# The last gate piece of a hybrid attention step, multiplied inside the first attention blocks

## The chip, the cores and the metric

The kernel runs on one core of one Trainium2 chip. The metric is device time in microseconds. The time before is 711.84 us, the median of three runs (711.51 to 711.89).

A core has five engines with a queue each. TensorE (PE in the profile) multiplies matrices into PSUM; its weight loads stand in a row of their own (PEld). VectorE (DVE), ScalarE (ACT) and GpSimd (POOL) do elementwise work; SyncE (SP) issues most of the transfers. Each engine takes its instructions in the order in which the program wrote them.

## The reference

One layer of a diffusion backbone for 128 context tokens and 1024 latent tokens, with 1024 channels. A normalized and modulated input h goes through one projection, whose columns are the queries, keys, values and gates of two mixers. Mixer A attends globally, mixer B in a window of 128 with a learned sink. Each mixer's output is multiplied by the SiLU of its gate, and both go through one output projection:

```
p = h @ w_in
q_a, k_a, v_a, g_a, q_b, k_b, v_b, g_b = jnp.split(p, SPLIT_IDX, axis=-1)
...
jnp.concatenate([o_a * jax.nn.silu(g_a), o_b * jax.nn.silu(g_b)], axis=-1) @ w_out
```

All of it is float32, and the kernel gets its accuracy by splitting an operand into a high and a low part: a product is then three matmuls (high x high, low x high, high x low).

## The kernel before

**Stages.** The kernel modulates and turns the input (h stays in SBUF as 2 x 3 x 8 pieces: high and low, three groups of tokens of 512, 256 and 384 columns, eight slices of 128 channels), multiplies the gates of mixer A, the queries, the keys and values, and then the gates of mixer B. After that comes the attention, with the output projection woven in.

**The gates of mixer B.** `gates` (L301) goes through 12 pieces: for each of the three token groups four pieces of 128 gate columns. A piece is 24 matmuls (`gate_products`, L253: eight slices times three) into one PSUM bank. `block` (L268) calls `tick` twice in a piece; `tick` (L131) runs what was put down with `later`. One tick behind its end a piece's SiLU runs on ScalarE, and SyncE stores the result in DRAM (`put_gates`, L286, into `g_dram`). The first four pieces are made at L842; the loop at L1060 makes the other eight. Beside these eight, at an even rate set in L1050, run 26 steps that find the score maxima of attention units 0 and 2 (L881, with the reduction on VectorE at L882), and the splits of w_out into high and low (`split_wo`, L1033) at set ticks (`WO_STEPS`, L53). The last gate piece holds the gate columns 384 to 511 of mixer B for the token columns 768 to 1151; the attention reads it for its last tokens only.

**The attention.** After a table load on ScalarE (L1069) the loop at L1262 goes through slots, here called blocks. A unit is one query tile, one mixer and one pair of heads. A unit of mixer A has nine blocks, one of mixer B three or four. Block s writes the scores of block s (`scores`, L1107) and the values of block s - 3 (`values`, L1134); between the two stand the steps that fall due: score maxima for a later unit of mixer A (L881), masked scores for the next unit of mixer B (L938 to L942, with their exponential at L928), weight splits, and products of the output projection (`out_items`, L1199), which start with block 23. In mixer A a block is: two matmuls for the scores (L1120, L1121), an exponential on ScalarE (L1123), the cast to the high part on ScalarE (L1127), the low part by a subtraction on GpSimd (L1131; every ninth on VectorE, L1129), and three matmuls with the values (L1141, L1143, L1144). In mixer B the weights are turned by four transposes (L1115), and cast and subtraction are L1116 and L1117.

**Buffers that make engines wait.** Scores alternate between two PSUM banks (tag B), score maxima, masked scores and small transposes between two others (tag A), the value sums between two (tag C); D and E belong to the output projection. A bank is free when its readers are done.

**The 1/denominator of mixer B** goes through a small reciprocal on VectorE (L977), a transpose on TensorE (L990), a copy on ScalarE (L994) and DRAM. For mixer A it is a logarithm and an exponential on ScalarE (L1155, L1156), one block after the unit's last value product, and the product on VectorE three blocks later (L1165).

**Places in SBUF.** The pieces of h are given up behind the gates, and w_out takes their places: `wo_big` and `spare` are the third group of tokens (L1030, L1074). The parts of w_out with the numbers 12 and 13 are loaded at blocks 8 and 9 and split three blocks later (`WO_LATE`, L51; loop L1266). `ogp` (L1079) holds the high and low parts of the gated outputs, five buffers each.

**Order.** `in_order` (L94) ties every instruction to the one before it on its engine, so the order of the code is that of the engines.

Of the kernel before, what the change touches and what calls it, by code (L numbers as in the profile page):

```python
# [9 lines left out]
F32 = mybir.dt.float32  # L10
F32R = mybir.dt.float32r
BF16 = mybir.dt.bfloat16
AF = mybir.ActivationFunctionType
ALU = mybir.AluOpType
# [4 lines left out]
P = 128  # L19
D = 1024  # L20
KT = D // P
# [26 lines left out]
MX_END = 10  # L48
SPLIT_LAG = 2

WO_LATE = {12: 8, 13: 9, 11: 21, 14: 22, 15: 23}  # L51

WO_STEPS = ((0, 4, 4), (1, 5, 5), (2, 6), (3, 7), (4, 8, 6), (5, 9), (6, 11), (7, 12, 10), (8, 13), (9, 14), (10, 16))  # L53
TURN = 2
# [9 lines left out]
NOG = 5  # L64
# [24 lines left out]
def place(t):  # L89

    return (t - 1) % NT
# [17 lines left out]
def hybrid_step(ctx, tc, x_prompt, x_sample, cache_k_a, cache_v_a, cache_k_b, cache_v_b,  # L109
# [3 lines left out]
    nc = tc.nc  # L113
# [6 lines left out]
    g_dram = dram.tile([16 * HD, TOK], F32, name="gd")  # L120
    gate_row = dram.tile([2, D], F32, name="gate_row")
# [5 lines left out]
    def later(n, f):  # L127

        agenda.setdefault(now[0] + n, []).append(f)

    def tick():  # L131
        now[0] += 1
        for f in agenda.pop(now[0], ()):
            f()
# [8 lines left out]
    def bank(tag, name):  # L143
        return ps.tile([P, 512], F32, tag=tag, name=name, bufs=BANKS[tag])
# [41 lines left out]
    def h_at(lo, i, k, to):  # L186
        c = k - k % GROUP[i]
        return h_tile[lo, i, c][:, k - c, to]
# [56 lines left out]
    W_GB = Weights([(CG[1], 512)], "gb")  # L245
# [20 lines left out]
    beside = [0.0, 0.0, []]  # L266
# [34 lines left out]
    def gates(w, m, nxt, thirds):  # L301

        pieces = [(ch, slice(a, b)) for a, b in thirds for ch in range(4)]
        for ch, ts in pieces:
            pg = bank_mm(f"pg{m}_{ch}_{ts.start}")[:, 0 : ts.stop - ts.start]
            block(pg, lambda k: gate_products(pg, w, ch, ts, k), nxt, nxt and (ch, ts) == pieces[-1])
            later(1, lambda pg=pg, ch=ch, ts=ts: put_gates(pg, m, ch, ts))
            yield
# [3 lines left out]
    with tc.tile_pool(name="st", bufs=2, side="right") as st:  # L312
# [79 lines left out]
        def keep(t, c, copy):  # L392
            at = slice(P * place(t), P * place(t) + P)
            copy(xT[:, 4 * c : 4 * c + 4, at], px.pop((t, c)).rearrange("p (k n) -> p k n", n=P))
# [72 lines left out]
        for j in range(1, KT + 2):  # L467
# [54 lines left out]
            if KT - 2 <= j < KT:  # L522
# [3 lines left out]
                c0, n = W_QA.cols[0]  # L526
# [50 lines left out]
    with tc.tile_pool(name="qt", bufs=2, side="right") as qt:  # L577
# [85 lines left out]
        for m in range(2):  # L663
            w, nxt = ((W_QA, W_QB), (W_QB, W_KV))[m]
            ts = list(range(1, NT)) + [0]
            for t in ts:
# [3 lines left out]
                if (m, t) in ((0, ts[-2]), (1, ts[GATE_AT[0]])):  # L670
                    n = len(wg) // 2
# [49 lines left out]
    with tc.tile_pool(name="kt", bufs=2) as kt:  # L721
# [117 lines left out]
        gb = gates(W_GB, 1, None, THIRDS)  # L839
# [166 lines left out]
    wo_raw, wo_parts, wo_big = {}, {}, {}  # L1006
# [3 lines left out]
    def h_slot(lo, i, c, name):  # L1010

        t = hp.tile([P, GROUP[i], THIRDS[i][1] - THIRDS[i][0]], F32R, tag=f"h{lo}{i}{c}", name=name)
        return t.rearrange("p k n -> p (k n)")

    def load_wo(i, pool=None):
        n, k = divmod(i, KT)
        if i in STAGE:
            wo_raw[i] = h_slot(*STAGE[i], f"wraw{i}").bitcast(F32)
        else:
            wo_raw[i] = pool.tile([P, 512], F32, tag="yt", name=f"wraw{i}")  # L1020
        nc.sync.dma_start(wo_raw[i], w_out[P * k : P * k + P, 512 * n : 512 * n + 512])

    def wo_place(lo, i):
        if i < 8:
            return h_slot(lo, 0, i, f"wo{lo}_{i}")
        if i < 12:
            return h_slot(lo, 1, 2 * (i - 8), f"wo{lo}_{i}")
        a, o = divmod(4 * lo + i - 12, 3)
        if a not in wo_big:
            wo_big[a] = h_slot(a // 2, 2, 4 * (a % 2), f"wo_big{a}")  # L1030
        return wo_big[a][:, 512 * o : 512 * o + 512]

    def split_wo(i):  # L1033
        raw = wo_raw.pop(i)
        hi, lo = (wo_place(j, i) for j in range(2))
        wo_parts[i] = hi, lo
        nc.vector.tensor_copy(hi, raw)
        (nc.gpsimd if i % 2 else nc.vector).tensor_tensor(lo, raw, hi, op=ALU.subtract)
# [8 lines left out]
    for i in EARLY:  # L1047
        items, end = max_items(i)
        beside[2] += items + [end]
    beside[:2] = 0.0, (len(beside[2]) + 0.5) / 64  # L1050
    def wo_step(i, *then):
        split_wo(i)
        for j in then:
            load_wo(j)
# [2 lines left out]
        load_wo(i)  # L1057
    for i, at, *then in WO_STEPS:
        later(at, lambda i=i, then=then: wo_step(i, *then))
    for n, _ in enumerate(gb):  # L1060
        if n == 4:
            for i in (7, 8, 9):
                load_wo(i)
    for f in beside[2]:
# [5 lines left out]
        name=nc.get_next_instruction_name(), engine=mybir.EngineType.Activation, act_func_set_id=6))  # L1070

    qp2.append(ctx.enter_context(tc.tile_pool(name="qp2", bufs=1, side="right")))
    w3 = ctx.enter_context(tc.tile_pool(name="w3", bufs=4, side="right"))
    spare = h_slot(1, 2, 4, "spare").bitcast(F32)  # L1074
    wo_big[2] = h_slot(1, 2, 0, "wo_big2")
    gate = spare[:, 0:512], wo_big[2].bitcast(F32)[:, 1024:1536]
    for n in range(2):
        nc.sync.dma_start(gate[n], gate_row[0:1, 512 * n : 512 * n + 512].to_broadcast([P, 512]))
    ogp = ctx.enter_context(tc.tile_pool(name="ogp", bufs=NOG, side="right"))  # L1079
    w2 = ctx.enter_context(tc.tile_pool(name="w2", bufs=2, side="right"))  # L1080
    def blocks(t, m, g):

# [13 lines left out]
    def load_gate(i):  # L1096
        if i < NU:
            t, m, g = units[i]
            sgl[i] = w2.tile([P, 2, P], F32, tag="sgl", name=f"sgl{i}")
            h0 = HD * (8 * m + 4 * g)  # L1100
            nc.sync.dma_start(
                sgl[i], g_dram[h0 : h0 + 4 * HD, P * place(t) : P * place(t) + P].rearrange("(c p) n -> p c n", p=P))
# [4 lines left out]
    def scores(i, b, blk):  # L1107

        t, m, g = units[i]
        s = bank("B", f"st{i}_{b}")  # L1110
        ph, pl = parts_tiles(i, b)
        if m == 1:
            o = P * blk[0]
            for h in range(4):
                nc.tensor.transpose(s[:, P * h : P * h + P], penat[i][:, h, o : o + P], ident_r.bitcast(F32))  # L1115
            nc.scalar.copy(ph, s)  # L1116
            later(1, lambda: nc.vector.tensor_tensor(pl, s, ph, op=ALU.subtract))  # L1117
            return ph, pl
        kh, kl = blk[0]
        nc.tensor.matmul(s, kh, qtile[i], start=True, stop=False)  # L1120
        nc.tensor.matmul(s, kl, qbtile[i], start=False, stop=True)  # L1121
        pe = w3.tile([P, 512], F32, tag="pe", name=f"pe{i}_{b}", bufs=PES)
        nc.scalar.activation(pe, s, AF.Exp)  # L1123
        if i == 0 and b < PH_DVE:
            nc.vector.tensor_copy(ph, pe)
        else:
            nc.scalar.copy(ph, pe)  # L1127
        if b in PL_DVE:
            later(1, lambda: nc.vector.tensor_tensor(pl, pe, ph, op=ALU.subtract))  # L1129
        else:  # L1130
            nc.gpsimd.tensor_tensor(pl, pe, ph, op=ALU.subtract)  # L1131
        return ph, pl
# [93 lines left out]
    slots, start = [], []  # L1226
# [29 lines left out]
            put(s, f)  # L1256
        put(end, done)

    credit, live = 0.0, []
    load_gate(0)  # L1260
    load_gate(1)
    for s in range(len(slots) + LAG + PROMPT_END[3]):  # L1262
        tick()
        if s < len(slots):
            live.append((slots[s], slots[s] and scores(slots[s][0], slots[s][1], slots[s][3])))
        for n, at in WO_LATE.items():  # L1266
            if s == at:
                load_wo(n, w2)
                later(3, lambda n=n: split_wo(n))
        for f in due.get(s, ()):  # L1270
            f()
        rate = OUTRATE if s < len(slots) and slots[s] else PADRATE
        credit = min(credit + rate, 6.0) if outq else 0.0
        while outq and credit >= 1.0:
            outq.pop(0)()
            credit -= 1.0
        if s >= LAG and live:
            slot, parts = live.pop(0)
            if slot:
                values(*slot, *parts)  # L1280
# [65 lines left out]
```

## Time and profile before

| what | value |
| --- | --- |
| median of three runs | 711.84 us |
| the profiled execution's own time | 711.52 us |
| span of the profile (first to last instruction) | 709.6 us |
| granted TensorE clock | 0.999 |
| TensorE busy | 691.6 us, 97% |
| VectorE, ScalarE, GpSimd busy | 66%, 58%, 47% |
| last gate piece of mixer B on TensorE | 298.60 to 303.12 us |
| first twelve blocks of the attention on TensorE | 303.12 to 321.90 us |

How to read it: the times of a timeline are counted from the span's start. A row gives the start, the duration, the engine, the line, the operation, what is written and read and its shape; in brackets stands how long the engine was idle just before and what ended that. A matmul's duration reaches over the start of the next one, since TensorE overlaps them. The rows that group a line give how often it ran and the shortest, the median and the longest duration in ns.

### The profile page before, as it was taken

The numbers are of one execution on the slowest core, as the hardware profiler recorded it, in microseconds if no ns is written. First come the engines' busy times: TensorE is split into PE (matmuls) and PEld (weight loads), VectorE is DVE, ScalarE is ACT, GpSimd is POOL, SyncE is SP. The second block draws the span as 40 slices with busy tenths as digits, with TensorE's granted clock in tenths as the row PEclk, the third lists the DMA queues.
The fourth block names the chain that finished last, engine by engine and source line by source line (L and its number), as shares of the span: only waits on it lengthen the run. The fifth ranks groups of instructions, "written<-read, shape, count | busy, mean of one in ns | idle before, by whom it ended". The sixth has DMA issues, their size and how long they took to land. (4 is left out here: it accounts for less than half of the span.)

```text
span 709.6 us, 10604 instructions
## 1 busy us (share of the span) xinstructions
PE 691.6 (97%) x3508; PEld 558.5 (79%) x3508; DVE 469.3 (66%) x1019; ACT 409.9 (58%) x829; POOL 334.2 (47%) x356
## 2 busy tenths in 40 slices
PE   7999999999999999989999999999999999999987
PEld 4778988878787889966788888888888888787865
DVE  4667257967848945647867578666775776675662
ACT  5646412412403431188777887787778777877760
POOL 3547023233213421256756655665576557555660
PEclk9999999999999999999999999999999999999999
DMA  8962283358353116332222121212221221222323
GB/s 316 415 211 102 78 302 74 90 154 263 84 139 104 37 39 215 123 108 57 78 68 85 50 82 53 71 57 75 68 82 38 79 71 50 78 72 70 104 67 121
DMA packets 53560, 78.58 MB, mean 111 GB/s; under 512 B 7096, under 2 KB 25720, under 8 KB 52608
## 3 DMA queue, kind: packets, MB, share of 16 engines
q1 hardware_dynamic: 45328, 65.96, 28.1%
q10 hardware_dynamic: 8176, 11.94, 6.3%
q8 instruction: 28, 0.46, 0.3%
q14 instruction: 28, 0.23, 0.1%
HBM read 58.69 MB, written 19.18 MB: 110 GB/s over the span
## 5 line engine op out<-in xcount | busy, mean ns | idle before, releaser
L1131 POOL TENSOR_TENSOR pl<-pe,ph 128x512 fp32r<-128x512 f32 x130 | 167.7, 1292 | 145.0 <-DVE nm L942 67.5
L882 DVE TENSOR_REDUCE mx<-pmx 128x1 f32<-128x384 f32 x192 | 101.4, 552 | 56.3 <-PE pmx L881 54.8
L1123 ACT ACTIVATE pe<-st 128x512 f32<-128x512 f32 x146 | 86.8, 594 | 28.2 <-PE st L1121 27.4
L1127 ACT CAST ph<-pe 128x512 fp32r<-128x512 f32 x146 | 90.6, 621 | 4.8
L1141 PE MATMUL pv<-ph,v_hi 128*128 128x512 f32 x208 | 82.8, 398 | 2.2 <-DVE spare L1165 2.2
L1144 PE MATMUL pv<-pl,v_hi 128*128 128x512 f32 x208 | 82.4, 396 | 0.0
L1212 PE MATMUL po<-wo,ogh 128*128 128x512 f32 x216 | 72.6, 395 | 0.2 <-DVE yt L1219 0.2
L174 POOL TENSOR_TENSOR rs_q<-ms_q,mhalf 128x8 f32<-128x8 f32 x18 | 34.1, 1896 | 80.9 <-DVE ms_q L172 80.9
L942 DVE CUSTOM_DVE_ANT_0 sn<-sn,mask,nsink 128x512 f32<-128x512 f32 (+1 forms) x64 | 46.4, 724 | 38.0 <-PE sn L939 37.6
L881 PE MATMUL pmx<-kha,qt 128*128 128x384 f32 x192 | 61.2, 363 | 0.4 <-ACT pen L928 0.2
L1120 PE MATMUL st<-qt,kha 128*128 128x512 f32 x144 | 58.2, 404 | 1.9 <-ACT pe L1123 1.1
L1121 PE MATMUL st<-qb,kla 68*128 68x512 f32 x144 | 57.5, 399 | 1.1 <-DVE qb L901 1.1
L1143 PE MATMUL pv<-ph,v_lo 128*64 128x512 f32 x146 | 57.6, 395 | 0.0
L1144 PEld LDWEIGHTS pv<-pl,v_hi 128*128 128x128 f32 x208 | 39.2, 189 | 16.4
L928 ACT ACTIVATE pen<-sn,nm 128x512 f32<-128x512 f32 (+2 forms) x72 | 45.0, 626 | 6.5 <-DVE nm L942 3.1
L1116 ACT CAST ph<-st 128x512 fp32r<-128x512 f32 x62 | 36.4, 587 | 19.9 <-PE st L1115 18.7
L1141 PEld LDWEIGHTS pv<-ph,v_hi 128*128 128x128 f32 x208 | 39.3, 189 | 10.6 <-ACT ogh L1177 2.4
L646 ACT CAST qo0q<-ptq 128x512 fp32r<-128x512 f32 x18 | 10.6, 586 | 60.7 <-PE ptq L643 55.8
L1212 PEld LDWEIGHTS po<-wo,ogh 128*128 128x128 f32 x216 | 40.0, 188 | 6.8 <-DVE yt L1219 0.6
L1117 DVE TENSOR_TENSOR pl<-st,ph 128x512 fp32r<-128x512 f32 x62 | 42.5, 686 | 2.7 <-ACT ph L1116 2.1
L1212 PE MATMUL po<-wo,ogl 128*128 128x512 f32 x108 | 42.6, 394 | 0.0
L881 PEld LDWEIGHTS pmx<-kha,qt 128*128 128x128 f32 x192 | 35.6, 191 | 6.4 <-DVE mx L882 1.3
(213 smaller groups left out, 1699.2 us busy)
## 6 DMA issues: line engine op xcount, KB each, us to landing
qt<-qd SPq DMA_DIRECT2D x36, 256.0 KB, 3.0
wm<-in_w_mod_ss_dram SPq DMA_DIRECT2D x7, 1024.0 KB, 10.0
qd<-qo0q ACTq DMA_DIRECT2D x36, 128.0 KB, 2.4
qd<-qo1q ACTq DMA_DIRECT2D x36, 128.0 KB, 2.4
sgl<-gd SPq DMA_DIRECT2D x36, 128.0 KB, 2.2
out_dram<-yt SPq DMA_DIRECT2D x17, 256.0 KB, 2.0
xn<-in_x_sample_dram SPq DMA_DIRECT2D x8, 512.0 KB, 7.2
wg<-in_w_mod_g_dram SPq DMA_DIRECT2D x4, 1024.0 KB, 8.3
```

Of the source, the lines that this page charges most:

```text
L881: nc.tensor.matmul(pm[:, 0:384], lhs, kha[:, g, 3 * b : 3 * b + 3, :], start=True, stop=True)
L882: nc.vector.tensor_reduce(mx[:, h, b : b + 1], pm[:, 0:384], axis=AX.X, op=ALU.max)
L942: nc.vector.tensor_tensor_reduce(s, s, mask[:, m0 : m0 + n], -1.0, nsink[:, 4 * g + h : 4 * g + h + 1], op0=ALU.add, op1=ALU.min, accum_ou ...
L1120: nc.tensor.matmul(s, kh, qtile[i], start=True, stop=False)
L1121: nc.tensor.matmul(s, kl, qbtile[i], start=False, stop=True)
L1123: nc.scalar.activation(pe, s, AF.Exp)
L1127: nc.scalar.copy(ph, pe)
L1131: nc.gpsimd.tensor_tensor(pl, pe, ph, op=ALU.subtract)
L1141: nc.tensor.matmul(pv, two, ph, start=(b == 0), stop=False)
L1143: nc.tensor.matmul(pv[0:64, :], vl, ph, start=False, stop=False)
L1144: nc.tensor.matmul(pv, two, pl, start=False, stop=last)
L1212: nc.tensor.matmul(po[n], a, wo_parts[KT * n + k][lo], start=(k == KS[0] and p == 0), stop=(k == KS[-1] and p == 2))
```

## The change

The last of the 12 gate pieces of mixer B is taken out of the gate stage. Its weights, 16 tiles of 128 x 128, are copied by ScalarE into buffers of `ogp`, which is opened earlier for that. Its 24 products are multiplied in the attention, four in each of the blocks 0 to 5, ahead of the block's value products, into a bank of tag D. The eight products with the low part of h come first, so that its places can be given to `spare` and `wo_big` in block 2, where now also the two gate rows are loaded. In block 6 ScalarE makes exp(-x) of the sum (256 and 128 columns). In blocks 7, 8 and 9 VectorE makes x / (1 + exp(-x)) for 128 columns each: an addition, a reciprocal, a product. SyncE stores the result in two transfers, in blocks 8 and 9. The parts 12 and 13 of w_out are loaded two blocks later, and so split two blocks later. The 26 steps beside the gates are spread over seven pieces in place of eight. Since the gate stage has two ticks fewer, the last of its weight splits (part 10) falls into block 0 of the attention.

```
-WO_LATE = {12: 8, 13: 9, 11: 21, 14: 22, 15: 23}
+WO_LATE = {12: 10, 13: 11, 11: 21, 14: 22, 15: 23}
+LATE_RATE = 4
+LATE_AT = (6, 7, 8, 9)
...
-    beside[:2] = 0.0, (len(beside[2]) + 0.5) / 64
+    beside[:2] = 0.0, (len(beside[2]) + 0.5) / 56
...
-    for n, _ in enumerate(gb):
+    ogp = ctx.enter_context(tc.tile_pool(name="ogp", bufs=NOG, side="right"))
+    kept = {}
+
+    def keep(k):
+        for lo, src in enumerate((W_GB.hi[k], W_GB.lo[k])):
+            if k % 2 == 0:
+                kept[lo, k // 2] = ogp.tile([P, 2, P], F32R, tag=("ogh", "ogl")[lo], name=f"kept{lo}_{k}")
+            nc.scalar.copy(kept[lo, k // 2][:, k % 2], src[:, 384:512])
+
+    for n in range(7):
+        next(gb)
+        if n == 3:
+            for k in range(KT):
+                later(1 + k // 2, lambda k=k: keep(k))
...
-    spare = h_slot(1, 2, 4, "spare").bitcast(F32)
-    wo_big[2] = h_slot(1, 2, 0, "wo_big2")
-    gate = spare[:, 0:512], wo_big[2].bitcast(F32)[:, 1024:1536]
-    for n in range(2):
-        nc.sync.dma_start(gate[n], gate_row[0:1, 512 * n : 512 * n + 512].to_broadcast([P, 512]))
-    ogp = ctx.enter_context(tc.tile_pool(name="ogp", bufs=NOG, side="right"))
+    spare, gate = None, None
+
+    def open_spare():
+        nonlocal spare, gate
+        spare = h_slot(1, 2, 4, "spare").bitcast(F32)
+        wo_big[2] = h_slot(1, 2, 0, "wo_big2")
+        gate = spare[:, 0:512], wo_big[2].bitcast(F32)[:, 1024:1536]
+        for n in range(2):
+            nc.sync.dma_start(gate[n], gate_row[0:1, 512 * n : 512 * n + 512].to_broadcast([P, 512]))
+
+    late_gate = []
+
+    def late_product(w, x, k, n):
+        if n == 8:
+            open_spare()
+        if n == 0:
+            late_gate.append(bank("D", "pgl")[:, 0:384])
+        nc.tensor.matmul(late_gate[0], kept[w, k // 2][:, k % 2], h_at(x, 2, k, slice(0, 384)), start=n == 0, stop=n == 23)
+        if n == 23:
+            for a, b, tag in ((0, 256, "ogh"), (256, 384, "ogl")):
+                late_gate.append((a, b, ogp.tile([P, 2, P], F32, tag=tag, name=f"sg{tag}").rearrange("p c n -> p (c n)")))
+
+    def late_exp():
+        for a, b, sg in late_gate[1:]:
+            nc.scalar.activation(sg[:, 0 : b - a], late_gate[0][:, a:b], AF.Exp, scale=-1.0)
+
+    def late_quotient(n):
+        a, b, sg = late_gate[1 + n // 2]
+        o = P * (n % 2)
+        nc.vector.tensor_scalar(sg[:, o : o + P], sg[:, o : o + P], 1.0, None, op0=ALU.add)
+        nc.vector.reciprocal(sg[:, o : o + P], sg[:, o : o + P])
+        nc.vector.tensor_tensor(sg[:, o : o + P], late_gate[0][:, a + o : a + o + P], sg[:, o : o + P], op=ALU.mult)
+        if a + o + P == b:
+            nc.sync.dma_start(g_dram[512 + 3 * P : 512 + 4 * P, 768 + a : 768 + b], sg[:, 0 : b - a])
+
+    lateq = [(0, 1, k) for k in (4, 5, 6, 7, 0, 1, 2, 3)] + [(w, 0, k) for k in range(KT) for w in range(2)]
+    lateq = [lambda n=n, a=a: late_product(*a, n) for n, a in enumerate(lateq)]
...
-    credit, live = 0.0, []
+    credit, live, late = 0.0, [], 0.0
...
+        if s in LATE_AT:
+            n = LATE_AT.index(s)
+            late_quotient(n - 1) if n else late_exp()
...
+        late += LATE_RATE
+        while lateq and late >= 1.0:
+            lateq.pop(0)()
+            late -= 1.0
```

## The prediction

> **What bounds the kernel now.** I read the page's first lines, then the stretches around the change (busy time by window), then the timelines of TensorE, ScalarE, VectorE and GpSimd there.
>
> ```profile
> span 709.6 us, 10604 instructions
> PE 691.6 (97%) x3508; PEld 558.5 (79%) x3508; DVE 469.3 (66%) x1019; ACT 409.9 (58%) x829; POOL 334.2 (47%) x356
> ```
>
> ```profile
> 298.60:303.12 4.52, 4.52 (x27) 4.43 (x27) 3.04 (x7) 0.49 (x1) 0.00 (x0) 1.00 0.22 76
> 303.12:321.90 18.78, 15.91 (x74) 10.95 (x72) 8.74 (x20) 16.83 (x35) 10.45 (x10) 1.00 0.34 98
> 365.00:640.00 275.00, 275.00 (x1326) 221.66 (x1326) 189.13 (x404) 217.14 (x431) 162.25 (x173) 1.00 0.22 68
> ```
>
> The columns behind the length are TensorE, its weight loads, VectorE, ScalarE, GpSimd. In the last gate piece (first row) TensorE has no gap. In the first twelve blocks of the attention (second row) it is idle for 2.87 of 18.78 us, and ScalarE, at 16.83 us, is the busiest. From 365 to 640 us TensorE is dense again, so whatever the opening gains or loses is carried to the end: the program order is fixed, and nothing later has slack to give it back.
>
> ```profile
> 298.60 0.33 PE L263 MATMUL pg<-h,whigb 128*128 128x384 f32 x1
> 298.77 0.34 PE L264 MATMUL pg<-h,wlogb 128*128 128x384 f32 x1
> ...
> 305.83 0.50 PE L1120 MATMUL st<-qt,kha 128*128 128x512 f32 x1 [0.80 <-ACT pe L1123]
> ...
> 307.05 0.44 PE L938 MATMUL sn<-khb,qt 128*128 128x384 f32 x1 [0.49 <-ACT pen L928]
> ...
> 308.76 0.44 PE L938 MATMUL sn<-khb,qt 128*128 128x384 f32 x1 [0.49 <-ACT pen L928]
> ...
> 312.66 0.50 PE L1120 MATMUL st<-qt,kha 128*128 128x512 f32 x1 [0.27 <-ACT pe L1123]
> ...
> 316.50 0.60 PE L1115 MATMUL st<-ident_r,pen 128*128 128x128 f32 x4
> ...
> 318.27 0.80 PE L881 MATMUL pmx<-kha,qt 128*128 128x384 f32 x2
> ...
> 320.45 0.39 PE L1143 MATMUL pv<-ph,v_lo 128*64 128x512 f32 x1
> 320.68 0.40 PE L1144 MATMUL pv<-pl,v_hi 128*128 128x512 f32 x1
> 321.90 0.47 PE L1120 MATMUL st<-qt,kha 128*128 128x512 f32 x1 [0.82 <-DVE pl L1117]
> ```
>
> The brackets are the waits. A 512-column matmul lasts 0.40 us but the next starts 0.23 us after it, so each wait also costs the 0.17 us of lost overlap: 2.87 + 5 x 0.17 = 3.7 us, and the first matmul behind a wait is up to 0.1 us longer (0.50 beside 0.40), 0.5 us in all. About 4.2 us is the most that filling TensorE's waits up to 321.90 can bring. A 384-column product starts 0.17 us after the one before.
>
> **The change, part by part.** I put zero at the first attention instruction (303.12 us before) and ask how far the new opening lags.
>
> *Removed:* 24 products. The piece takes 4.52 us, of which two score-maximum matmuls take 2 x 0.17 and move to earlier pieces; 4.18 us go, all on the path. The opening starts 4.18 us earlier. Its ScalarE start moves with it: a SiLU and the table load stand there as before, only of the piece ahead.
>
> ```profile
> 303.37 0.49 ACT L290 ACTIVATE sg<-pg 128x384 f32<-128x384 f32 x1 [4.21 <-PE ptm L900]
> 303.88 1.28 ACT L1069 ACT_TABLE_LOAD   x1
> ...
> 314.43 0.58 ACT L1123 ACTIVATE pe<-st 128x512 f32<-128x512 f32 x1
> 315.04 0.62 ACT L1127 CAST ph<-pe 128x512 fp32r<-128x512 f32 x1
> 315.56 0.59 ACT L1123 ACTIVATE pe<-st 128x512 f32<-128x512 f32 x1
> ...
> 321.11 0.59 ACT L1155 ACTIVATE rs<-pv 64x512 f32<-64x512 f32 x1 [0.23 <-PE pv L1144]
> ...
> 322.64 0.60 ACT L1123 ACTIVATE pe<-st 128x512 f32<-128x512 f32 x1 [0.27 <-PE st L1121]
> ```
>
> The 16 copies of the kept weights run on ScalarE in the gate stage, where it waited 4.21 us for each piece: nothing.
>
> *Added to TensorE:* four products (0.70 us) in each of blocks 0 to 5. ScalarE's chain in blocks 0 to 3 is full and does not move, so the matmul of 308.76, which waits for it, stays at 5.64. From there TensorE has no wait left: that pair (0.45), 12 products (2.09), nine value and six score matmuls (15 x 0.233 = 3.50); the last of these starts 0.23 before the sum, at 11.45, and ends at 11.85. The exponential of block 6 started at 11.31 (314.43) and now starts at 11.90. TensorE meets the transposes of block 9 at 14.89 instead of 13.38 (316.50): 1.51 late. If nothing more were late, the last value product of unit 0 would lag 1.92 (another 0.4 behind two maxima of block 10).
>
> *Added to ScalarE:* two exponentials behind the cast of block 6 (13.03 to 13.43, and 0.55 us of ScalarE in all, from 0.49 us for the 384-column SiLU). Not on the path by themselves, since TensorE already lags.
>
> *Added to VectorE:* three times an add, a reciprocal and a product on 128 columns. This is where I expect the gain to go.
>
> ```profile
> L895 DVE TENSOR_SCALAR m_nat<-m x16: 170/420/855, 285.0 to 648.5; 128x4 fp32r<-128x4 f32 x16
> ```
>
> ```profile
> 338.79 0.85 DVE L895 TENSOR_SCALAR m_nat<-m 128x4 fp32r<-128x4 f32 x1
> ```
>
> ```profile
> 314.49 1.29 POOL L1131 TENSOR_TENSOR pl<-pe,ph 128x512 fp32r<-128x512 f32 x1 [1.42 <-ACT ph L1127]
> ...
> 335.83 3.78 POOL L1131 TENSOR_TENSOR pl<-pe,ph 128x512 fp32r<-128x512 f32 x3
> ```
>
> ```profile
> L977 DVE RECIPROCAL inv<-sum x18: 166/168/179, 316.5 to 681.5; 128x4 f32<-128x4 f32 x18
> L892 DVE TENSOR_REDUCE m<-mx x16: 153/155/166, 284.8 to 648.4; 128x4 f32<-128x12 f32 x16
> L172 DVE TENSOR_SCALAR ms_k<-ssk x9: 170/170/171, 213.8 to 252.4; 128x4 f32<-128x4 f32 x9
> L718 DVE TENSOR_TENSOR v_lo<-pk,v_hi x9: 270/274/293, 215.6 to 253.8; 128x128 fp32r<-128x128 f32 x9
> ```
>
> L895 is the new add's form (SBUF to SBUF, float32, a constant). Alone it takes 0.17; at 338.79 it took 0.85 and ended at 339.64, when the third of GpSimd's subtractions ended (335.83 + 3.78 = 339.61). I read this as: such an add waits until GpSimd's running operation is done. Its price is 0.25 plus 0 to 1.29 us. Here the case is nearly fixed: GpSimd's subtraction of block 6 and the exponential both start when the same cast ends, the subtraction runs from 13.17 to 14.46, the first add is ready at 13.48 and ends at 14.70. The multiply reads PSUM; I give it L718's 0.28. The reciprocal of 128 columns stands in no row. On 4 columns it costs what an add costs (168 and 170), which makes 0.28 on 128, the low end; if its fixed part were the smallest here (L892: 155 less 12 columns at about 1 ns, 142), 26 ns would be left for 4 columns, 6.5 ns each, 0.97 us on 128, the high end. I take 0.28, since its fixed part should rather be that of the add, the nearest row; nothing below it, since no operation on 128 columns is shorter by more than some hundredths.
>
> With 0.05 between dependent steps the first part ends at 15.36. The second add meets block 7's subtraction (14.86 to 16.15): 16.39, and the part ends at 17.05. Queued behind it on VectorE: the maximum of block 8 (to 17.54), the small reciprocal L977 (17.62), the third part (GpSimd idle; 18.56), the maximum of block 9 (19.05). TensorE's transpose L990 needs L977: it waits from 16.12 to 17.67. The first maximum matmul of block 10 needs the PSUM bank that the maximum of block 9 releases: it starts at 19.10, where before it started at 15.15 (318.27). A wait of 0.2 us of before falls away there, so the last value product of unit 0 lags 3.77. ScalarE's logarithm L1155 follows it and the chain behind that is ScalarE's; of the lag its idle 0.27 us (322.64) is given back, and 0.2 comes on top, because two weight splits that VectorE did in blocks 11 and 12 (behind the wait of 0.82 at 321.90, which goes) now lie in blocks 13 and 14, where one cast meets GpSimd again. Sum: -4.18 + 3.77 - 0.27 + 0.2 = **-0.5 us**.
>
> *Moved:* the gate loads and two new stores on SyncE's queue.
>
> ```profile
> DMA to landing us min/median/max: 2.6/4.2/5.8
> ```
>
> That row is of the w_out loads. The stores wait for VectorE until about 18.6; behind them are the 1/denominator store of block 10, which waits for its own copy at 18.3 anyway, and from about 18.8 the two loads for the moved weight splits, which before had been issued at once. VectorE wants the first at 23.2; landed at 21.4 to 24.6, at the median 23.0. I take nothing; at the longest, VectorE is held 1.4 us with the block's mask sum behind it, and that belongs to the forecast's own range. One split of w_out slides to the first block; VectorE ends it at 0.7 and TensorE needs the bank behind it at 2.1.
>
> The profiled execution took 711.52 us beside a median of 711.84 of the three runs shown; it stands for them. Forecast 711.84 - 0.5 = **711.3 us**. A measurement of this kernel can tell about 0.2%, 1.4 us.
>
> **Rivals.** *The cover holds.* If the adds do not wait for GpSimd, each part takes 1.0 us, the maximum of block 9 ends at 17.3, and the lag at the last value product is 1.92: -4.18 + 1.92 - 0.27 - 0.2 = -2.7 us, 709.1. For it: the reciprocal L977 at 316.48 was not held up by GpSimd's run below.
>
> ```profile
> 316.48 0.17 DVE L977 RECIPROCAL inv<-sum 128x4 f32<-128x4 f32 x1
> ```
>
> ```profile
> 315.89 3.77 POOL L1131 TENSOR_TENSOR pl<-pe,ph 128x512 fp32r<-128x512 f32 x3
> ```
>
> Against it: the add's own form reaches 855 ns. Chance 0.22.
>
> *VectorE's queue in blocks 7 to 9 becomes the bound (slower).* The reciprocal enters three times, and behind it stand L977 and the maximum that frees TensorE's bank. At 0.97 us: 3 x 0.69 = 2.07 more, less 0.69 that the second add no longer waits: +1.38, that is +0.9 us, 712.7. The kernel is slower than before from about 0.52 us for a reciprocal. With a fixed part of 135 ns, 5% under the smallest row, it is 8.3 ns per column and 1.2 us; from about 1.05 us on, a further add starts just inside a subtraction of GpSimd and waits 1.25 us more: +2.3 to +2.6, 714.1 to 714.4. For it: the 4-column row cannot exclude several ns per column. Against: an add of 4 columns costs as much. Chance 0.30. [...]
>
> *The change only moves work.* TensorE gets 24 products less in one place and 24 more in another; if the opening were as dense as 365 to 640 us, the time would be 711.8. The idle 2.87 us speaks against it. Chance 0.06.
>
> **How the numbers follow.** Forecast 0.42, its own range 710.6 to 712.0 (0.7 us for the replay's rounding and alignment). Faster by over 0.2%: the first rival and a tenth of the forecast, 0.26. Slower by over 0.2%: three quarters of the second rival, and a few hundredths of the rest, 0.26. Within: 0.48. The range goes from 709.0, just under the first rival, to 714.0, which leaves out the far end of the second.
>
> **What would show it.** Right: the attention's first score matmul 4.2 us earlier; no wait of TensorE in blocks 4 to 9; adds of the new SiLU at 0.8 us or more, ending with a GpSimd subtraction; a wait of over 1 us at L990's transpose and another at a maximum matmul of block 10; the 0.82 wait before block 12 gone. Wrong: adds at 0.25 us (then -2.7), or a 128-column reciprocal of 0.9 us or more (then a loss). If the attention does not start 4.2 us earlier, the first term falls.

## The result and the profile after

The changed kernel takes 714.33 us, the median of eleven executions (712.35 to 716.27), beside 711.84 us for the kernel before, run next to it on the same chip (711.16 to 712.79, also eleven). The ratio is 1.0025 with an interval of 1.0013 to 1.0037: slower, and outside the forecast's range. The profiled execution took 714.81 us.

The first lines of the changed kernel's page. The nine more instructions on VectorE are the new SiLU's; the 17 more on ScalarE are the 16 copies and two exponentials, less the one SiLU that is gone; TensorE has as many as before.

```profile
span 712.9 us, 10632 instructions
PE 693.3 (97%) x3508; PEld 559.7 (79%) x3508; DVE 474.5 (67%) x1028; ACT 413.4 (58%) x846; POOL 335.3 (47%) x356
```

The busy time by window of the changed kernel, in the columns of the prediction: the first twelve blocks, the stretch up to the first score of unit 4, and the dense rest.

```profile
300.51:324.09 23.58, 20.86 (x97) 16.68 (x96) 13.60 (x30) 16.75 (x35) 10.56 (x10) 0.93 0.30 88
324.09:344.85 20.76, 19.64 (x88) 13.71 (x87) 15.98 (x36) 17.10 (x36) 15.61 (x16) 1.00 0.24 73
368.00:640.00 272.00, 272.00 (x1312) 218.93 (x1311) 188.50 (x401) 214.04 (x424) 159.75 (x170) 1.00 0.22 67
```

The opening lasts 23.58 us and not 18.78, and although the 24 products lie in it, TensorE is idle for nearly as long as before (2.72 beside 2.87 us). The third row shows that nothing is given back later, and the sixth figure behind the length, the granted clock, is 0.93 in the opening. The attention starts at 300.51, only 2.61 us earlier than at 303.12.

TensorE's timeline of the changed kernel, from the transpose of unit 0's maxima in the gate stage to block 12. (Lines have shifted: L1106 are the late products, L1166 and L1167 the scores, L1187 to L1190 the values, L992 the small transpose, L883 the score maxima, L902 the maxima's transpose.)

```profile
286.09 0.22 PE L902 MATMUL ptm<-ident_r,m_nat 128*4 128x128 f32 x1 [0.80 <-DVE mx L884]
300.51 0.23 PE L902 MATMUL ptm<-ident_r,m_nat 128*4 128x128 f32 x1
301.43 0.86 PE L1106 MATMUL pgl<-h,kept 128*128 128x384 f32 x4
304.44 0.44 PE L940 MATMUL sn<-khb,qt 128*128 128x384 f32 x1 [0.17 <-ACT pen L930]
318.58 0.27 PE L992 MATMUL pti<-ident_r,inv 128*4 128x128 f32 x1 [1.70 <-DVE inv L979]
320.47 0.69 PE L883 MATMUL pmx<-kha,qt 128*128 128x384 f32 x1 [0.84 <-DVE mx L884]
320.95 0.63 PE L1187 MATMUL pv<-ph,v_hi 128*128 128x512 f32 x1
321.38 0.63 PE L1189 MATMUL pv<-ph,v_lo 128*64 128x512 f32 x1
323.86 0.39 PE L1190 MATMUL pv<-pl,v_hi 128*128 128x512 f32 x1
324.09 0.40 PE L1166 MATMUL st<-qt,kha 128*128 128x512 f32 x1
```

Three things stand here. The waits for ScalarE are all but filled (0.17 where 0.80 and 0.49 stood). Two waits for VectorE have come, 1.70 and 0.84 us, at the small transpose and in block 10 as the prediction said (there on the second of the block's two maximum matmuls, 320.47, and not on the first), and the wait of 0.82 ahead of block 12 is gone. And two things stand here that the prediction did not have: a wait of 0.80 in the gate stage, and value matmuls that start 0.43 us apart at 320.95 and 321.38, where 0.23 is their rate elsewhere. The next rows, by window, show that as the clock.

```profile
316.50:319.98 3.48, 1.43 (x8) 0.66 (x6) 3.34 (x9) 1.18 (x3) 1.30 (x2) 1.00 0.11 38
319.98:323.39 3.41, 2.92 (x9) 2.42 (x10) 2.56 (x5) 0.01 (x1) 0.00 (x0) 0.50 0.50 164
323.40:326.00 2.60, 2.60 (x13) 2.16 (x13) 2.05 (x5) 2.22 (x4) 0.00 (x0) 1.00 0.51 163
```

For 3.41 us TensorE was granted half its clock, from 319.98 on, which lies inside the second wait (319.63 to 320.47); in the 3.48 us before, it had been busy for 1.43.

VectorE's timeline shows what TensorE waited for: add (L1118), reciprocal (L1119) and product (L1120), three times, with the maximum and the small reciprocal L979 between them.

```profile
313.94 1.13 DVE L1118 TENSOR_SCALAR sgogh<-sgogh 128x128 f32<-128x128 f32 x1 [2.55 <-ACT sgogh L1113]
315.10 0.95 DVE L1119 RECIPROCAL sgogh<-sgogh 128x128 f32<-128x128 f32 x1
316.19 0.29 DVE L1120 TENSOR_TENSOR sgogh<-pgl,sgogh 128x128 f32<-128x128 f32 x1
316.40 0.26 DVE L1118 TENSOR_SCALAR sgogh<-sgogh 128x128 f32<-128x128 f32 x1
316.69 0.95 DVE L1119 RECIPROCAL sgogh<-sgogh 128x128 f32<-128x128 f32 x1
...
317.89 0.55 DVE L884 TENSOR_REDUCE mx<-pmx 128x1 f32<-128x384 f32 x1
318.35 0.17 DVE L979 RECIPROCAL inv<-sum 128x4 f32<-128x4 f32 x1
318.44 0.20 DVE L1118 TENSOR_SCALAR sgogl<-sgogl 128x128 f32<-128x128 f32 x1
318.67 0.95 DVE L1119 RECIPROCAL sgogl<-sgogl 128x128 f32<-128x128 f32 x1
319.66 0.29 DVE L1120 TENSOR_TENSOR sgogl<-pgl,sgogl 128x128 f32<-128x128 f32 x1
319.87 0.55 DVE L884 TENSOR_REDUCE mx<-pmx 128x1 f32<-128x384 f32 x1
```

The same time on GpSimd:

```profile
313.69 1.29 POOL L1177 TENSOR_TENSOR pl<-pe,ph 128x512 fp32r<-128x512 f32 x1 [0.35 <-ACT ph L1173]
315.29 2.51 POOL L1177 TENSOR_TENSOR pl<-pe,ph 128x512 fp32r<-128x512 f32 x2 [0.31 <-ACT ph L1173]
```

The reciprocal takes 0.95 us on 128 columns. The first add takes 1.13 us and ends at 315.07, when GpSimd's subtraction (to 314.98) is done. The second (0.26) falls where one of the next two subtractions ends and the other begins; the third (0.20) comes behind both, when GpSimd is idle.

### The profile page after: what moved, and what is told of

It is laid out like the page before. It is cut to its first block, busy times and chain, and to the rows that moved or that the text cites. A ratio compares the mean times of both kernels' runs of the same rounds, so it can differ in the third digit from the quotient of the medians.

```text
span 712.9 us, 10632 instructions
## 1 busy us (share of the span) xinstructions
PE 693.3 (97%) x3508; PEld 559.7 (79%) x3508; DVE 474.5 (67%) x1028; ACT 413.4 (58%) x846; POOL 335.3 (47%) x356
## 5 line engine op out<-in xcount | busy, mean ns | idle before, releaser
L1187 PE MATMUL pv<-ph,v_hi 128*128 128x512 f32 x208 | 83.0, 399 | 1.9 <-DVE spare L1211 1.8
L1190 PE MATMUL pv<-pl,v_hi 128*128 128x512 f32 x208 | 82.5, 397 | 0.0
L883 PE MATMUL pmx<-kha,qt 128*128 128x384 f32 x192 | 61.9, 366 | 1.4 <-DVE mx L884 1.0
L1167 PE MATMUL st<-qb,kla 68*128 68x512 f32 x144 | 57.5, 399 | 1.1 <-DVE qb L903 1.1
L1166 PE MATMUL st<-qt,kha 128*128 128x512 f32 x144 | 57.7, 401 | 0.0
L1190 PEld LDWEIGHTS pv<-pl,v_hi 128*128 128x128 f32 x208 | 39.3, 189 | 16.7 <-issue 0.2
L1187 PEld LDWEIGHTS pv<-ph,v_hi 128*128 128x128 f32 x208 | 39.5, 190 | 10.3 <-ACT ogh L1223 2.5
L883 PEld LDWEIGHTS pmx<-kha,qt 128*128 128x128 f32 x192 | 35.8, 192 | 7.8 <-DVE mx L884 2.7
```

The lines of the kernel that those rows point to most:

```text
L883: nc.tensor.matmul(pm[:, 0:384], lhs, kha[:, g, 3 * b : 3 * b + 3, :], start=True, stop=True)
L1187: nc.tensor.matmul(pv, two, ph, start=(b == 0), stop=False)
L1190: nc.tensor.matmul(pv, two, pl, start=False, stop=last)
```

## The experiments

The theory after the result: VectorE's queue in blocks 7 to 9 makes the two waits, by the reciprocal's 0.95 us and the add's wait for GpSimd; the rest is the clock behind the waits and the wait of 0.80 in the gate stage. The rivals: the products or the two new stores themselves, the moved weight splits, or a loss anywhere else in the opening. All ratios are against the kernel before, run beside each; its median there was 711.77 to 712.05 us.

**The quotient left out.**

```
-        nc.vector.tensor_scalar(sg[...], sg[...], 1.0, None, op0=ALU.add)
-        nc.vector.reciprocal(sg[...], sg[...])
-        nc.vector.tensor_tensor(sg[...], late_gate[0][...], sg[...], op=ALU.mult)
```

> Leaves out the nine VectorE operations of the late SiLU (addition, reciprocal, product); what is stored for that gate piece is exp(-x). Theory (VectorE's queue in blocks 7 to 9 is the bound): TensorE's waits of 1.70 us at the small transpose and 0.84 us at a maximum matmul of block 10 go, the granted clock stays at full speed there, and the kernel is faster than before: the piece's 4.18 us less, 0.97 lost at unit 0's transpose in the gate stage, about 1.5 lost in the opening: 711.8 - 1.7 = 710.1 us (709.5 to 710.7). Rival (the 24 products and the two exponentials cost the time themselves): the waits stay or move to another place, and the time is 711.8 or more.

Measured: 709.7 us (709.02 to 712.43), ratio 0.9971 (0.9957 to 0.9986). The small transpose in the profile has no wait any more:

```profile
316.11 0.27 PE L992 MATMUL pti<-ident_r,inv 128*4 128x128 f32 x1
```

So the nine operations cost 4.5 us of the median (3.8 by the two ratios), and the products, copies, stores and moved splits together do not make the loss.

**Only the reciprocal left out, and only the add left out.** The first drops the middle line above, the second the first line.

> Leaves out the three reciprocals of 128 columns; the gate piece stored is x * (1 + exp(-x)). Theory (three terms share VectorE's queue: the reciprocals at 0.95 us, and additions that wait until GpSimd's running subtraction ends): the first addition still takes about 1.1 us, the second now meets the next subtraction and takes about 1.2 us, so that of the 3 x 1.0 us only about 1.5 us come off the last maximum of block 9; waits of about 0.7 us at the small transpose and up to 0.8 us behind it, time 711.2 us (710.5 to 712.2) with a full clock. Rival (the reciprocals are all of it): the waits of TensorE go, and the time is that of the run without the nine operations, about 710.1 us.

> The changed kernel without the three additions of 1; the gate piece stored is x / exp(-x). Theory (the first addition costs 1.13 us because it waits for GpSimd's subtraction, the others 0.2 to 0.3): 1.13 + 0.26 + 0.20 and the steps between, about 1.7 us, come off VectorE's queue; reciprocals do not wait for GpSimd; TensorE's waits of 1.70 and 0.84 us become about 0.3 and 0.8, and the time is 1.4 to 1.7 us under that of the changed kernel at equal clock: 712.4 us median (711.0 to 713.0), shortest execution 710.8. Rival (the reciprocal waits in the addition's place): the first reciprocal takes 1.8 us or more, and the time falls by 0.5 us at most.

Without the reciprocal: 711.01 us (710.38 to 712.44), ratio 0.9983 (0.9972 to 0.9994). Without the add: 711.03 us (710.55 to 712.17), ratio 0.9988 (0.9977 to 0.9998). VectorE's timeline of the kernel without the reciprocal:

```profile
313.17 1.13 DVE L1118 TENSOR_SCALAR sgogh<-sgogh 128x128 f32<-128x128 f32 x1 [2.55 <-ACT sgogh L1113]
...
314.65 1.25 DVE L1118 TENSOR_SCALAR sgogh<-sgogh 128x128 f32<-128x128 f32 x1
...
316.69 0.43 DVE L1118 TENSOR_SCALAR sgogl<-sgogl 128x128 f32<-128x128 f32 x1
```

and of the kernel without the add:

```profile
313.21 0.95 DVE L1118 RECIPROCAL sgogh<-sgogh 128x128 f32<-128x128 f32 x1 [2.56 <-ACT sgogh L1113]
...
314.51 0.94 DVE L1118 RECIPROCAL sgogh<-sgogh 128x128 f32<-128x128 f32 x1
...
316.24 0.92 DVE L1118 RECIPROCAL sgogl<-sgogl 128x128 f32<-128x128 f32 x1
```

The same first place in the queue costs an add 1.13 us and a reciprocal 0.95, its usual price: the add waits for GpSimd, the reciprocal does not. Without the reciprocal the second add moves into the next subtraction and waits too (1.25). The waits of TensorE shrink to 0.72 and 0.43 us in the one and to 0.22 and 0.57 in the other. Each edit gives back about 3.2 us of the median and the two together 4.5, not 6.4. The two waits, 2.54 us in the changed kernel, fall to 1.15 and to 0.79, which counts 0.6 us of them twice. The clock is 1.00 in both profiles, and its mean is 0.997 or more in every execution of both kernels: either edit alone seems to keep the clock up, so that this gain, too, is counted twice.

**The transpose in the gate stage one tick later.** 

```
-            later(TURN, transpose)
+            later(TURN + (i == 0), transpose)
```

> The transpose that carries the maxima of unit 0 (gate stage) comes one tick later; nothing else. Theory (it now comes too early for VectorE, because the 26 steps lie closer): TensorE's wait of 0.80 us there goes, 0.97 us with the lost overlap; the attention starts 0.97 us earlier against the piece ahead, and the time is about 1.0 us under that of the changed kernel: 713.3 us, if the clock behaves alike. Rival (VectorE is behind anyway and the wait moves to the next matmul of a maximum): no wait at the transpose, one of up to 0.8 us at a maximum matmul, and 714.3 us.

Measured: 713.31 us (711.22 to 714.25), ratio 1.0013 (1.0 to 1.0025). The wait of 0.80 is gone, and 1.0 us of the median with it. The intervals of the two kernels overlap, but the profiles show the same: from the first product of the gate stage to the attention it is 51.64 us here (247.07 to 298.71) and 52.57 in the changed kernel (247.94 to 300.51). In TensorE's timeline the transpose, the two waits for VectorE, and the last value product of unit 0:

```profile
286.72 0.22 PE L902 MATMUL ptm<-ident_r,m_nat 128*4 128x128 f32 x1
...
316.78 0.27 PE L992 MATMUL pti<-ident_r,inv 128*4 128x128 f32 x1 [1.72 <-DVE inv L979]
...
318.67 0.44 PE L883 MATMUL pmx<-kha,qt 128*128 128x384 f32 x1 [0.84 <-DVE mx L884]
...
320.73 0.40 PE L1190 MATMUL pv<-pl,v_hi 128*128 128x512 f32 x1
```

The waits of 1.72 and 0.84 us are there, and yet the clock stays at 1.00 (the sixth figure behind the length):

```profile
315.00:316.70 1.70, 0.06 (x1) 0.00 (x0) 1.67 (x5) 0.05 (x1) 1.00 (x1) 1.00 0.00 0
316.70:318.60 1.90, 1.05 (x6) 0.66 (x6) 1.83 (x6) 0.84 (x2) 0.00 (x0) 1.00 0.20 69
318.60:322.00 3.40, 3.33 (x17) 2.71 (x18) 3.21 (x8) 1.39 (x3) 0.00 (x0) 1.00 0.55 189
```

So half the clock does not follow from the waits every time. What it costs where it does follow can be read from the same work in the two profiles: from the waiting maximum matmul to the last value product it is 2.06 us here (318.67 to 320.73) and 3.39 in the changed kernel (320.47 to 323.86), 1.33 us more.

**The changed kernel once more**, unaltered, for a second profile.

> The changed kernel itself, unaltered, for a second profile and for executions on the same chip as the other runs. Theory (the waits of 1.70 and 0.84 us belong to the kernel, the 3.4 us at half clock behind them only to some executions): both waits are there to 0.05 us, a stretch of half clock may or may not be; median 713.0 to 714.5 us, the shortest execution about 712.4. Rival (the half clock follows the waits in each execution): it stands at the same place in this profile too.

Measured: 714.09 us (712.28 to 716.26), ratio 1.0021 (1.0007 to 1.0035). The waits are 1.72 and 0.84 us in this profile, and half the clock is granted for 3.41 us in the same place:

```profile
317.00:318.90 1.90, 1.05 (x6) 0.66 (x6) 1.83 (x6) 0.84 (x2) 0.00 (x0) 1.00 0.20 69
319.08:322.49 3.41, 3.19 (x10) 2.67 (x11) 2.30 (x6) 0.27 (x1) 0.00 (x0) 0.50 0.53 174
322.50:324.00 1.50, 1.50 (x8) 1.23 (x7) 1.14 (x2) 1.02 (x3) 0.00 (x0) 1.00 0.80 241
```

**The waits filled with constant matmuls.** They bring VectorE's results no earlier; they only keep TensorE busy while it waits. First the small transpose's wait alone, then both waits, together with the transpose one tick later.

```
+            if i == 1:
+                idle = bank("E", "fill")
+                for _ in range(7):
+                    nc.tensor.matmul(idle, ident_b, ident_b..., start=True, stop=True)
```

> Seven matmuls of constants (512 columns each, 1.6 us in all) stand ahead of the small transpose of unit 1, where TensorE waited 1.70 us; they write a PSUM bank that nobody reads. Theory (the wait lets the granted clock fall to half for one stretch of 3.4 us, in some executions): the matmuls cost nothing, the clock is full in every execution (0.999 or 1.000 where the changed kernel had 0.992 to 1.000), the executions lie close together, and the median falls from 714.3 to 712.6 us (712.3 to 713.0). Rival (the spread has another cause, the place of the wait does not matter for it): the executions spread over 712.4 to 716.3 as before, the median stays at 714.3, or rises with the added matmuls by up to 1.6 us.

> As the run with seven matmuls of constants ahead of the small transpose, with three more ahead of the second maximum matmul of block 10 (the wait of 0.84 us), and with unit 0's transpose one tick later. Theory (both waits together let the granted clock fall): the waits are filled, so that no execution loses clock there; the executions above the lowest by more than 1.2 us become as rare as in the kernel before (about one in three), and the median is 711.4 us (711.0 to 711.9), the shortest execution level of the run with the later transpose (711.2) plus at most 0.3. Rival (the spread comes from elsewhere): the median stays at 712.5 to 713.3 us with half the executions above 712.5.

The first wait filled: 713.09 us (711.92 to 715.04), ratio 1.0012 (0.9998 to 1.0026); eight of the twelve executions lie above 713, and in this kernel's profile the wait of 0.84 us is left; the theory held at most in part. Both filled, with three such matmuls ahead of the maximum: 711.8 us (711.08 to 712.74), ratio 0.9995 (0.9982 to 1.0008), and none of the twelve executions above 712.74. TensorE's timeline of that kernel:

```profile
315.41 1.69 PE L998 MATMUL fill<-ident_b 128*128 128x512 bf16 x7
...
317.27 0.27 PE L1000 MATMUL pti<-ident_r,inv 128*4 128x128 f32 x1 [0.18 <-DVE inv L983]
...
318.17 0.82 PE L879 MATMUL fill<-ident_b 128*128 128x512 bf16 x3
...
319.17 0.44 PE L887 MATMUL pmx<-kha,qt 128*128 128x384 f32 x1 [0.17 <-DVE mx L888]
```

By the medians ten matmuls that compute nothing make the kernel 1.5 us faster than the one with the later transpose alone (713.31; 1.3 by the two ratios, whose intervals overlap), and its spread falls from 3.0 to 1.7 us. VectorE's results come no earlier, so the gain is most likely the clock's: the mean granted clock of the twelve executions is 0.997 to 0.999, where with the later transpose alone it goes down to 0.994. Both profiles grant 1.00 behind the waits, so that the traces of these two kernels do not show the difference; in this one:

```profile
318.00:322.00 4.00, 3.83 (x19) 2.53 (x20) 3.96 (x9) 1.53 (x3) 0.00 (x0) 1.00 0.41 140
```

With 1.0 us for the transpose and 1.4 to 1.5 for the clock, the changed kernel's 714.2 (714.33 and 714.09 in its two sets) becomes 711.8. Without these two losses the kernel is level with the one before, to within the interval (1.3 us faster to 0.6 slower).

**The moved weight splits alone**, in the kernel before.

```
-WO_LATE = {12: 8, 13: 9, 11: 21, 14: 22, 15: 23}
+WO_LATE = {12: 10, 13: 11, 11: 21, 14: 22, 15: 23}
```

> The kernel before with one part of the change alone: the parts 12 and 13 of w_out are loaded and split two blocks later. Theory (the wait of 0.82 us ahead of block 12 comes from the splits queued on VectorE ahead of block 10's low part): the wait goes, some of it comes back where the splits now lie, about 0.5 us are gained: 711.3 us beside 711.8. Rival (the wait has another cause): it stays, 711.8 us.

Measured: 712.33 us (711.39 to 714.27), ratio 1.0006 (0.9995 to 1.0017): no gain, the expectation failed. TensorE's waits from 250 to 372 us in this profile have the 0.82 ahead of block 12 no more, but those of the masked scores are longer, 1.4 us in four places, where before they were 1.0 in two (in a row: us in all, how many, the longest):

```profile
PE sn L938 <- ACT pen L928: 1.4, 4, 0.5
PE st L1120 <- ACT pe L1123: 1.1, 2, 0.8
```

The wait was a place where a lag could be taken back, not time to be had by itself.

**The SiLU on ScalarE.** exp(-ln(1 + exp(-x))) in place of the add and the reciprocal; VectorE keeps the product alone. The transpose goes one tick later, too.

```
...
+            if n == 0:
+                nc.scalar.activation(sg, sg, AF.Ln, bias=1.0)
+            elif n == 1:
+                nc.scalar.activation(sg, sg, AF.Exp, scale=-1.0)
+            else:
+                nc.vector.tensor_tensor(sg, late_gate[0][:, a:b], sg, op=ALU.mult)
```

> The late SiLU without additions and reciprocals on VectorE: in block 7 ScalarE takes the logarithm of 1 + exp(-x), in block 8 the exponential of minus that, and in block 9 VectorE makes the product alone (256 and 128 columns); unit 0's transpose in the gate stage comes one tick later. Theory (VectorE's queue was the bound; ScalarE has room behind block 8): no wait of TensorE at the small transpose, the level of the run without the nine operations (709.7 us) less 0.97 for the transpose plus up to 1 us, because ScalarE is given four instructions of about 0.25 us each in blocks 7 and 8: 709.3 us (708.6 to 710.0). Rival (ScalarE becomes the bound in blocks 7 and 8): waits of TensorE for the exponential or the cast of blocks 8 to 10, 710.5 us or more.

> As the run before, but the logarithm in block 9, the exponential in block 10 and the products in block 11, where ScalarE was idle for 1 us and more a block. Theory: the four instructions cost nothing there: 709.7 - 0.97 = 708.7 us (708.2 to 709.4), under the run with blocks 7 to 9 or equal to it. Rival (they hold up the cast of block 10 or 11, which frees TensorE's bank): a wait of about 0.5 us at block 12 and a time above that run's.

With the logarithm in block 7: 709.74 us (709.17 to 710.41), ratio 0.9961 (0.9947 to 0.9974); ScalarE's copy of the 1/denominators comes later, and TensorE waits for it once:

```profile
317.09 0.74 PE L883 MATMUL pmx<-kha,qt 128*128 128x384 f32 x2 [0.65 <-ACT spare L996]
```

With the three steps in blocks 9, 10 and 11: 709.06 us (708.28 to 711.48), ratio 0.9959 (0.9946 to 0.9973), and no new wait at all.

**Another pace for the products** in that kernel: three a block, with the SiLU two blocks later, or six a block.

```
-LATE_RATE = 4
+LATE_RATE = 6
```

> The version with the SiLU on ScalarE in blocks 9 to 11, with three products a block in blocks 0 to 7 in place of four in blocks 0 to 5, and the exponentials of -x in block 8. Theory (what is left of the opening's loss is TensorE coming 0.5 to 0.6 us late to block 6): block 6's exponential comes less late, the same 24 products, and the time is that of the version with four or up to 0.4 us less: 708.9 us (708.4 to 709.4). Rival (fewer products early leave the waits of blocks 2 and 3 open): waits there grow by up to 0.4 us, 709.4 us.

> The same version with six products a block in blocks 0 to 3. Theory: TensorE comes late to the scores of blocks 3 and 4, ScalarE, which is full there, has to wait, and the whole opening moves by that: 709.6 us (709.2 to 710.2). Rival (ScalarE is ahead far enough): the time of the version with four, 709.0.

Three a block: 709.36 us (708.66 to 712.44), ratio 0.9971 (0.9958 to 0.9984), with a wait of 0.48 us for ScalarE in block 2, as the rival said, where four a block left 0.17. Six a block: 708.21 us (707.89 to 709.24), ratio 0.9949 (0.9931 to 0.9966), where I had expected a loss; my theory fell. With four a block ScalarE still ran out of scores ahead of block 6's exponential, as its timeline in the kernel with 709.06 us shows:

```profile
311.07 0.60 ACT L1171 ACTIVATE pe<-st 128x512 f32<-128x512 f32 x1 [0.45 <-PE st L1169]
```

With six a block the products are done in block 3 (the last six start at 305.50), where ScalarE has no gap; TensorE catches up before block 6, and no such bracket stands in its ScalarE timeline until 317.21 (0.71). This is the fastest kernel of the study, 3.6 us under the kernel before in the medians run side by side. The intervals of the three paces overlap, so that their order among themselves is not settled.

## Why the prediction was wrong, point by point

- **The steps that failed.** The sum gave -0.5 us, and the two profiled spans differ by +3.3. Of these 3.8 us, 0.6 was lost before the gate stage starts (247.94 us beside 247.35), where the change does nothing; the second profile of the changed kernel starts it at 246.77, so that this belongs to the execution. The rest are three steps of the sum and its tail: the clock, which had no term (1.3), the 26 steps, moved at no cost (1.0), VectorE's queue with the reciprocal in it (0.7), and the tail (0.2).
- **The clock** is the largest. In the profile before it is 1.00 throughout the opening. In both profiles of the changed kernel two waits of 1.7 and 0.84 us with 1.05 us of work between them were followed by 3.41 us at half clock; in that of the later transpose they were not. The sum had both waits and gave them no price beyond their length.
- **"The opening starts 4.18 us earlier."** It started 2.61 earlier, 3.20 counted from the start of the gate stage. The missing 0.97 is the transpose of unit 0's maxima (0.80 and the 0.17 of lost overlap): the 26 steps, over seven pieces, end only just ahead of it. The later transpose gave this back.
- **"I take 0.28, since its fixed part should rather be that of the add, the nearest row".** The reciprocal of 128 columns took 0.95 us. With 0.17 on 4 columns that is (0.95 - 0.17) / 124 = 6.3 ns per column, beside 0.97 and 6.5 ns at the stated high end. The 4-column row could not tell a fixed price from a price per column, and the two ends lay on the two sides of zero. The far end of the second rival, 8.3 ns per column and 1.2 us, no run shows; 6.3 and 0.95 is what was measured.
- **"The last value product of unit 0 lags 3.77."** From the attention's start it is at 23.35 us (323.86 - 300.51) beside 17.56 before, 5.79 late and 2.02 more than the sum had. 1.33 of that is the clock, as read above. The other 0.7 is VectorE's queue: the maximum of block 9 ends at 19.91 where the sum had 19.05. The three reciprocals are 3 x 0.67 = 2.0 dearer, but the second add takes 0.26 where the sum had 0.98 behind a subtraction, and the other steps together some 0.4 less; and since the wait fell on the second maximum matmul of block 10, some 0.2 of the 0.86 would have passed in any case. So the wrong price of the reciprocal was partly paid by the add, and VectorE's queue as measured, put into the sum alone, turns it from -0.5 to about +0.2.
- **The tail, -0.27 + 0.2.** Measured about +0.1: the lag at the last value product, -2.61 + 5.79 = 3.18 us, is 3.3 in the span.
- **Luck:** the rival's sum, 712.7, lies among the four shortest executions (712.35 to 712.78, with mean granted clocks of 0.997 to 1.0). But these paid 0.97 for the transpose, which that sum did not have, and it priced VectorE's queue at 1.38 more than the forecast, where 0.7 was measured. With the transpose later and the waits filled the kernel takes 711.8, level with the one before.
- **Right:** the place and the mechanism; the add waits for the end of GpSimd's operation (1.13; 1.25 for the second without the reciprocal), so the first rival falls; the wait at the small transpose (predicted 1.55, measured 1.70) and one in block 10; four products at 0.69 to 0.70 us a block; the exponential of block 6 at 11.86 us from the attention's start, 0.55 late where 0.59 stood; the wait of 0.82 gone. That the change only moves work is out: without the SiLU's nine operations it gains 2.2 us.

**Open:** about one in three executions of the kernel before lies above 712.5 us, and a few of the best versions are as far above their median; no profile here caught one, so where they lose it is not shown. On what the fall of the clock behind the two waits depends is open, too.

## What to carry to other kernels

The price of an operation that has been seen only on a few columns can be read as a fixed one or as one per column (the reciprocal took 0.17 us on 4 columns and 0.95 on 128): when the two readings put the sum on the two sides of zero, the sign of the change is not known. A wait of TensorE can cost more than its length, by the clock behind it (1.33 us here, behind waits of 1.70 and 0.84). Steps pressed closer together can come ahead of the engine that they read (a wait of 0.80 us here, with the 26 steps over seven pieces). Before work is moved into an engine's gaps, list who reads that engine's queue behind it: TensorE had the room here, VectorE was busy for only 66% of the span, and still three short dependent chains in front of a maximum and a 1/denominator cost about as much as the piece that was moved (4.5 us of the median beside 4.18). Put filler work where the other engine is the bound (blocks 0 to 3; finishing it early cost nothing here: 708.21 us with six products a block, 709.06 with four), and give the elementwise rest to an engine whose queue nobody waits for at that moment.

## What the runs showed of the hardware

- TensorE's clock fell to half for 3.41 us in both profiles of the changed kernel, in the first behind a stretch of 3.48 us in which it had been idle for 2.05, made of one wait and the first 0.35 us of a second, with work between them. With the later transpose the same two waits (1.72 and 0.84) are there, and its profile shows no half clock; what decides between the two no run shows.
- On VectorE a float32 reciprocal of 128 columns takes 0.92 to 0.95 us. It runs beside a GpSimd subtraction without waiting (0.95 us from 313.21 on in the kernel without the add, where GpSimd subtracts from 312.98 to 314.27); an add with a constant, from SBUF to SBUF, waits until that subtraction is done (0.20 us with GpSimd idle, 0.43, 1.13 and 1.25 when caught in one).
- With the two waits filled, the executions lay within 1.7 us; with one or both open, in the kernels that have all nine operations, within 3.0 to 4.0. The waits are not all that spreads them: the kernel before, which has neither, lay within 3.3 to 4.6 us in the three later sets. Its 29 executions above 712.5 us there have a mean granted clock of 0.995, the other 62 one of 0.997.
